# The last output bank of an encoder kernel in two column halves, and tile 2's scaling behind the last square root

## The chip, the cores and the metric

The kernel runs on one core of one Trainium2 chip. The metric is the device time of one execution in microseconds. Before the change three runs gave 1183.38, 1183.96 and 1184.81 us; their median, 1183.96, is the time before. The engines are named as in the profile: PE is TensorE's matmuls and PEld its weight loads, DVE is VectorE, ACT is ScalarE, POOL is GpSimd and SP is SyncE, which only issues DMAs here. ACT issues DMAs too.

## The reference

A two-layer pre-norm encoder on 512 tokens (an 8 by 64 grid) of width 1024, all in float32. Layer 0 mixes with two kinds of attention, layer 1 with a neighbourhood attention; each layer ends in a squared-ReLU MLP of width 4096, and the whole in an RMSNorm. Only the end matters here:

```python
def rmsnorm(x, g):
    xf = x.astype(jnp.float32)
    y = xf * lax.rsqrt(jnp.mean(xf * xf, axis=-1, keepdims=True) + EPS)
    return (y * g.astype(jnp.float32)).astype(x.dtype)

def sq_relu_mlp(h, w_up, w_down):
    u = jax.nn.relu(h @ w_up)
    return (u * u) @ w_down
...
        h = h + sq_relu_mlp(rmsnorm(h, norm_ffn[layer]), ffn_w_up[layer], ffn_w_down[layer])
    return rmsnorm(h, final_norm)
```

## The kernel before

A float32 product is made from three matmuls in a faster type: each operand is split into a high and a low part, and high times high, high times low and low times high are added up in PSUM. Most of the kernel keeps the activations transposed, features on partitions, in a tile called hT.

The end of the last MLP is different. Of its 32 blocks of 128 hidden features, the last four are not multiplied in the transposed form: they are kept back (V) and used as the stationary operand, so that the product comes out with tokens on partitions, which is how the output is stored and how the last norm sums its squares along a row. `last_mlp` does this. H holds four tiles, H[0] to H[3], each of 128 tokens by 1024 columns; G holds the final gain on all partitions; ss is a 128 x 8 tile with the sums of squares, column j for the first 512 columns of tile j and column 4 + j for the last 512.

`down(k0, c, up, tail)` makes column half c of all four tiles. It takes four PSUM banks of 128 x 512, and `use(k, j)` adds the three matmuls of hidden block k to bank j (L1627 to L1629). With c = 0, two blocks go over all four banks in turn and the last two blocks bank by bank; with c = 1 all four blocks go bank by bank, so bank 0 is finished first and bank 3 last, each after 12 matmuls of 512 columns. When a bank is finished, `add` (L1581, VectorE) adds it to H[j].

For c = 0, `first_half` then sums the squares (L1585, ScalarE, with an accumulator that a short instruction reads out), makes 1/D times the sum plus EPS in ss (L1589, VectorE) and multiplies the half by the gain (L1590, VectorE). For c = 1, `last_half` sums the squares of the second half (L1585) and finishes the tile:

- L1595, ScalarE: root, the square root of the whole mean
- L1596, VectorE: v, the mean itself
- L1597, VectorE: y, the reciprocal of the root
- L1599 to L1601, VectorE: one Newton step, a factor rf for each token
- L1603 and L1604, ScalarE: the first 512 columns times rf, then their store to DRAM (256 KB), issued from ScalarE's queue
- L1605, VectorE, and L1606, SP: the last 512 columns times rf times the gain, then their store, issued from SP's queue

Each engine takes its instructions from its own queue in a fixed order. A scheduler sets that order when the program is built, from the program's text and its dependencies; between instructions of one engine it may change the order of the text. `tc.keep_in_program_order` marks an instruction that it leaves where the text has it. Instructions of different engines wait for each other by semaphores. Around the last bank, the queue of VectorE had these in this order: L1605 of tile 1; L1596, L1597 and L1599 of tile 2; the add of tile 3 (L1581); L1600, L1601 and L1605 of tile 2; L1596 and the rest of tile 3. ScalarE's had: L1595 of tile 2; the store L1604 of tile 1; the squares of tile 3; L1603 of tile 2; L1595 of tile 3; the store of tile 2; L1603 and the store of tile 3.

Of the kernel before, what the change touches and what calls it, by code (L numbers as in the profile page):

```python
# [11 lines left out]
AF = mybir.ActivationFunctionType  # L12
ALU = mybir.AluOpType
# [3 lines left out]
S = 512  # L17
D = 1024
# [17 lines left out]
def encoder_kernel(ctx: ExitStack, tc: tile.TileContext, ins, out, dbg=None):  # L36
    nc = tc.nc
    PE, ACT, DVE, POOL, SP = nc.tensor, nc.scalar, nc.vector, nc.gpsimd, nc.sync
# [40 lines left out]
    def mmb():  # L79
        return bank("mm", 3)  # L80

    def sbk():
        return bank("s", 2)

    def stb():
        return bank("t", 2)

    def ob():
        return bank("o", 1)

    def scratch(dt=F32):
        return scp.tile([P, 512], dt, tag="sc", name=nm("sc"))

    def tiny(n, dt=F32):
        return tp.tile([P, n], dt, tag=f"ti{n}", name=nm("ti"))

    def keep(shape, dt, name):
        return big.tile(shape, dt, tag=name, name=name)
# [127 lines left out]
    def rows(w, k0, nk):  # L226
        return w[k0 * P : (k0 + nk) * P, :].rearrange("(k p) n -> p k n", p=P)
# [5 lines left out]
    def plan(*spec, make=None):  # L233
        asked.append((make or chunk, spec))
        return len(asked) - 1

    def weights(i, ahead=AHEAD):
        while len(loaded) < min(i + LOAD + 1, len(asked)):
            make, spec = asked[len(loaded)]
            loaded.append(make(*spec))  # L240
            next(loaded[-1])
        while len(ready) < min(i + ahead + 1, len(asked)):
            hi, lo, lows = next(loaded[len(ready)])
            ready.append((hi, lo))
            low_parts.append(lows)

            give_low(len(ready) - fixed[0])
        give_low(i + 1)
        return ready[i]
# [4 lines left out]
    def give_low(n):  # L254
        while given[0] < n:
            for z in low_parts[given[0]]:
                z()
            given[0] += 1
# [147 lines left out]
    def group(n):  # L406

        flip[0] ^= 1
        if flip[0]:
            return [sbk(), stb(), stb(), ob()][:n]  # L410
        return [mmb(), mmb(), mmb(), sbk()][:n]
# [232 lines left out]
    hold = {}  # L644
# [65 lines left out]
    banks = [mmb() for _ in range(3)] + [sbk(), sbk(), ob()]  # L710
# [860 lines left out]
    def last_mlp():  # L1571
        H = []
        G = []
        ss = keep([P, 8], F32, "ss")
        ov = out.rearrange("b (r c) d -> (b c) r d", r=ROWS)

        def half(j, c):
            return H[j].t[:, S * c : S * c + S]

        def add(j, c, b):  # L1580
            DVE.tensor_tensor(half(j, c), half(j, c), b, op=ALU.add)  # L1581

        def squares(j, c):
            sq = scratch()
            ACT.activation(sq, half(j, c), AF.Square, accum_out=ss[:, 4 * c + j : 4 * c + j + 1])  # L1585

        def first_half(j):
            squares(j, 0)
            DVE.tensor_scalar(ss[:, j : j + 1], ss[:, j : j + 1], 1.0 / D, EPS, op0=ALU.mult, op1=ALU.add)  # L1589
            DVE.tensor_tensor(half(j, 0), half(j, 0), G[0].t[:, 0:S], op=ALU.mult)  # L1590

        def last_half(j):
            squares(j, 1)
            v, root, a, y, rf = (tiny(1) for _ in range(5))
            ACT.activation(root, ss[:, 4 + j : 5 + j], AF.Sqrt, bias=ss[:, j : j + 1], scale=1.0 / D)  # L1595
            DVE.tensor_scalar(v, ss[:, 4 + j : 5 + j], 1.0 / D, ss[:, j : j + 1], op0=ALU.mult, op1=ALU.add)  # L1596
            DVE.reciprocal(y, root)  # L1597

            DVE.tensor_scalar(a, v, y, y, op0=ALU.mult, op1=ALU.mult)  # L1599
            DVE.tensor_scalar(a, a, -0.5, 1.5, op0=ALU.mult, op1=ALU.add)  # L1600
            DVE.tensor_tensor(rf, a, y, op=ALU.mult)  # L1601
            dst = ov[16 * j : 16 * j + 16]
            ACT.activation(half(j, 0), half(j, 0), AF.Copy, scale=rf)  # L1603
            ACT.dma_start(dst[:, :, 0:S], half(j, 0))  # L1604
            DVE.scalar_tensor_tensor(half(j, 1), half(j, 1), rf, G[0].t[:, S:], op0=ALU.mult, op1=ALU.mult)  # L1605
            SP.dma_start(dst[:, :, S:], half(j, 1))  # L1606

        def turn(i, c):

            b = stb() if flip[0] == 0 else mmb()  # L1610
            for q in range(4):
                PE.transpose(b[:, q * P : (q + 1) * P], hT[:, 4 * c + q, i * P : (i + 1) * P], ident)
            ACT.activation(half(i, c), b, AF.Copy)

        def down(k0, c, up, tail):

            nk = len(up)
            ids = [plan([(0, S, rows(ins["ffn_w_down"][1], k0 + k, 2)[:, :, S * c : S * c + S])], 2, S)
                   for k in range(0, nk, 2)]

            def run():
                banks = group(4)

                def use(k, j):
                    wh, wl = (x[:, k % 2, :] for x in weights(ids[k // 2]))
                    uh, ul = (up[k][:, z, j * P : (j + 1) * P] for z in range(2))
                    PE.matmul(banks[j], uh, wh, start=k == 0, stop=False)  # L1627
                    PE.matmul(banks[j], uh, wl, start=False, stop=False)
                    PE.matmul(banks[j], ul, wh, start=False, stop=k == nk - 1)  # L1629

                for k in range(nk - tail):
                    for j in range(4):
                        use(k, j)
                for j in range(4):
                    for k in range(nk - tail, nk):
                        use(k, j)
                    if c == 0:
                        turn(j, 1)
                    add(j, c, banks[j])
                    (first_half, last_half)[c](j)  # L1640
                    if c == 0 and j == 3:

                        ACT.activation(tiny(1), ones[:, 0:1], AF.Sqrt)

            return run

        runs, V = [], []

        def last(k0, tiles_):
            V.extend(tiles_)  # L1650
            up = [s_.pair() for s_ in V]
            runs.extend(down(k0, c, up, 2 + 2 * c) for c in range(2))

            def beside(m, i):
                if m == 2 and i == 0:
                    H.extend(Slot(F32) for _ in range(4))
                    G.append(Slot(F32))
                    SP.dma_start(G[0].t, ins["final_norm"].unsqueeze(0).to_broadcast([P, D]))
                if m > 1 and i in (16, 22):
                    turn(2 * (m - 2) + (i == 22), 0)  # L1660

            return beside

        mlp(1, last)
        for run in runs:
            run()
        for s_ in V:
            s_.free()

    last_mlp()  # L1670


# [50 lines left out]
```

## Time and profile before

| what | value |
|---|---|
| median of three runs | 1183.96 us (1183.38 to 1184.81) |
| the profiled execution's own time | 1184.41 us |
| its span, first to last instruction | 1182.3 us |
| PE matmul, busy | 1162.6 us, 98% |
| PE weight load, busy | 1018.3 us, 86% |
| VectorE, busy | 877.6 us, 74% |
| ScalarE, busy | 640.0 us, 54% |
| GpSimd, busy | 520.1 us, 44% |
| mean granted TensorE clock | 0.997 |

A profile comes from one execution. Its times count from the start of its span, in us. A timeline row gives start, duration, engine, line, operation and its tiles; a bracket at its end tells how long the engine was idle before and what released it. ACTq and SPq rows are an engine's queue issuing a DMA. The chain of waits is followed back from the last instruction of a compute engine: each row is a piece of time and what filled it, and "issue" is time in which the engine waited for nothing that the profile shows. Grouped rows give a line, its tiles and shapes, the count, then the busy time in us and the mean ns of one, then the idle time before. Rows over stretches of time give, for each stretch, its length, the busy time of each engine with its number of instructions, the granted PE clock, the busy share of the DMA engines and their GB/s. DMA rows give, per queue, packets, MB and the busy share in that stretch. The end of a matmul is modelled and matmuls overlap; the rate is read from their starts.

### The profile page before, as it was taken

What the parts mean: (1) busy time and instruction counts of PE and PEld (TensorE: products, weight loads), DVE (VectorE), ACT (ScalarE), POOL (GpSimd) and SP (SyncE); (2) the same over time, 40 slices, a digit from 0 to 9 for tenths busy, and PEclk for the clock granted to TensorE, in tenths of its full rate; (3) what the DMA queues carried; (4) which work ended last, traced back from release to release, by engine and by line L of the source; (5) the groups of instructions that cost most, each with busy time, mean ns of one, the idle gap of its engine ahead of it and who ended that gap; (6) DMA issues with size and microseconds to landing.
All of it is one profiled execution on the core that took longest, in us unless ns stands there. A gap on an engine that the chain in (4) does not pass through costs nothing.

```text
span 1182.3 us, 19765 instructions
## 1 busy us (share of the span) xinstructions
PE 1162.6 (98%) x7128; PEld 1018.3 (86%) x7128; DVE 877.6 (74%) x1506; ACT 640.0 (54%) x1081; POOL 520.1 (44%) x659
## 2 busy tenths in 40 slices
PE   9999999999999999999999999999999999999997
PEld 8667788887899899988998998988889989998895
DVE  5588998878967378786984676667995736777975
ACT  5577676764446246662543555555544524666344
POOL 3257242215662477709502232231366625774820
PEclk9999999999999999999999999999999999999998
DMA  7223314222515722225226574443352332322412
GB/s 245 73 58 92 86 54 135 72 63 81 177 56 152 253 72 82 72 91 169 63 76 174 137 180 126 115 112 109 106 162 81 116 126 62 90 72 90 143 37 71
DMA packets 110145, 128.01 MB, mean 108 GB/s; under 512 B 9075, under 2 KB 86816, under 8 KB 110048
## 3 DMA queue, kind: packets, MB, share of 16 engines
q1 hardware_dynamic: 106992, 119.30, 33.9%
q0 software_dynamic: 2304, 6.31, 2.3%
q10 hardware_dynamic: 752, 1.15, 0.3%
q8 instruction: 56, 0.92, 0.3%
q14 instruction: 41, 0.34, 0.1%
HBM read 104.32 MB, written 6.29 MB: 94 GB/s over the span
## 4 chain that ended last, share of the span: by engine, by line
PE 86%; DVE 7%; ACT 3%; issue 1%; POOL 1%; DMA 1%; SPq 0%; DVEq 0%; ACTq 0%; POOLq 0%
PE mm L503 8%; PE mm L501 8%; PE mm L502 8%; PE mm L390 3%; PE mm L389 3%; PE mm L388 3%; PE s L503 3%; PE s L501 3%; PE s L502 3%; PE t L389 3%; PE t L388 3%; PE t L390 3%; PE s L991 2%; PE s L390 2%; PE s L388 2%; PE s L389 2%
## 5 line engine op out<-in xcount | busy, mean ns | idle before, releaser
L309 DVE TENSOR_TENSOR wlo<-a,whi 128x896 fp32r<-128x896 f32 x132 | 164.5, 1251 | 83.6 <-ACT whi L308 82.8
L308 ACT ACTIVATE whi<-a 128x896 fp32r<-128x896 f32 x132 | 124.7, 949 | 152.3 <-PE o L502 45.9
L501 PE MATMUL mm<-a,whi 128*128 128x512 f32 x485 | 195.5, 405 | 0.2 <-DVE hT L925 0.2
L503 PE MATMUL mm<-a,wlo 128*128 128x512 f32 x485 | 191.9, 397 | 2.4 <-DVE wlo L202 2.4
L502 PE MATMUL mm<-a,whi 128*128 128x512 f32 x485 | 192.2, 396 | 0.1
L202 DVE TENSOR_TENSOR wlo<-raw,whi 128x1024 fp32r<-128x1024 f32 (+4 forms) x117 | 139.3, 1194 | 69.6 <-ACT whi L212 66.1
L212 ACT ACTIVATE whi<-raw 128x1024 fp32r<-128x1024 f32 (+3 forms) x120 | 116.3, 970 | 99.2 <-PE s L502 32.1
L302 POOL TENSOR_TENSOR a<-a 128x128 f32<-128x128 f32 x132 | 84.0, 636 | 171.4 <-DMA a<-in_ffn_w_up_dram 98.9
L304 POOL TENSOR_TENSOR a<-a 128x128 f32<-128x128 f32 x132 | 122.6, 928 | 10.3
L303 POOL TENSOR_TENSOR a<-a 128x256 f32<-128x256 f32 x132 | 117.5, 890 | 10.3
L503 PEld LDWEIGHTS mm<-a,wlo 128*128 128x128 f32 x485 | 91.0, 188 | 25.0 <-DVE wlo L202 2.9
L501 PEld LDWEIGHTS mm<-a,whi 128*128 128x128 f32 x485 | 91.2, 188 | 20.3 <-issue 1.4
L502 PEld LDWEIGHTS mm<-a,whi 128*128 128x128 f32 x485 | 91.4, 189 | 19.6 <-issue 1.7
L389 PE MATMUL mm<-a,whi 128*128 128x256 f32 x370 | 104.1, 281 | 0.0
L388 PE MATMUL mm<-a,whi 128*128 128x256 f32 x370 | 103.9, 281 | 0.0
L390 PE MATMUL mm<-a,wlo 128*128 128x256 f32 x370 | 103.8, 281 | 0.0
L999 POOL TENSOR_SCALAR p<-p,ti 128x512 f32<-128x512 f32 x64 | 46.1, 721 | 88.5 <-DVE ti L998 74.5
L1424 POOL TENSOR_SCALAR p<-p,ti 128x256 f32<-128x256 f32 x64 | 35.4, 564 | 105.7 <-DVE ti L1423 92.6
L388 PE MATMUL t<-a,whi 128*128 128x256 f32 x264 | 74.2, 281 | 0.0
L389 PE MATMUL t<-a,whi 128*128 128x256 f32 x264 | 74.2, 281 | 0.0
L390 PE MATMUL t<-a,wlo 128*128 128x256 f32 x264 | 73.9, 280 | 0.0
L390 PEld LDWEIGHTS mm<-a,wlo 128*128 128x128 f32 x370 | 69.7, 188 | 0.2 <-DVE wlo L309 0.2
(333 smaller groups left out, 3195.1 us busy)
## 6 DMA issues: line engine op xcount, KB each, us to landing
a<-in_ffn_w_up_dram SPq DMA_DIRECT2D x104, 256.0 KB
raw<-in_ffn_w_down_dram SPq DMA_DIRECT2D x46, 512.0 KB
raw<-in_od_w_qkv_dram SPq DMA_DIRECT2D x64, 128.0 KB
a<-in_ffn_w_down_dram SPq DMA_DIRECT2D x28, 256.0 KB
raw<-in_ffn_w_up_dram SPq DMA_DIRECT2D x12, 512.0 KB
raw<-in_ev_w_in_dram SPq DMA_DIRECT2D x12, 384.0 KB
a<-a SPq DMA_DIRECT2D x18, 256.0 KB
bias<-bx SPq DMA_DIRECT2D x16, 256.0 KB
```

Of the source, the lines that this page charges most:

```text
L202: z = lambda: (eng or DVE).tensor_tensor(to, src, f32(high), op=ALU.subtract)
L212: ACT.activation(hi[:, 0:m], raw[:, 0:m], AF.Copy)
L303: POOL.tensor_tensor(r[:, 4:6], r[:, 2:3].to_broadcast([P, 2, P]), r[:, 0:7:6], op=ALU.add)
L304: POOL.tensor_tensor(r[:, 7], r[:, 3], r[:, 5], op=ALU.subtract)
L308: ACT.activation(hi[:, 0:896], raw[:, 128:1024], AF.Copy)
L309: DVE.tensor_tensor(lo[:, 0:896], raw[:, 128:1024], f32(hi[:, 0:896]), op=ALU.subtract)
L388: PE.matmul(o, wh, x[:, 0], start=kp == 0 and n in (0, 1, 3, 5), stop=False, skip_group_check=True)
L389: PE.matmul(o, wh, x[:, 1], start=False, stop=False, skip_group_check=True)
L390: PE.matmul(o, wl, x[:, 0], start=False, stop=kp == self.np - 1, skip_group_check=True)
L501: PE.matmul(o, wh, xh, start=first, stop=False)
L502: PE.matmul(o, wh, xl, start=False, stop=False)
L503: PE.matmul(o, wl, xh, start=False, stop=last)
```

## The change

Two things are changed, both for the last bank, c = 1 and j = 3. The bank is made in two halves of 256 columns: all 12 matmuls for columns 0 to 255, then all 12 for columns 256 to 511, and after each half `last_bank` adds that half to H[3] and sums its squares. After the first half a new one-column step on VectorE adds the first sum to ss[3], so that the second sum can be written over it. And tile 2's `last_half` stops after rf: its two scalings and its two stores (`store`) are called after tile 3's `scale`, which holds the square root; the ScalarE scaling of tile 2 is marked to stay there.

```diff
-        def add(j, c, b):
-            DVE.tensor_tensor(half(j, c), half(j, c), b, op=ALU.add)
+        def add(j, c, b, o=0, n=S):
+            h = half(j, c)[:, o : o + n]
+            DVE.tensor_tensor(h, h, b[:, o : o + n], op=ALU.add)
 
-        def squares(j, c):
+        def squares(j, c, o=0, n=S):
             sq = scratch()
-            ACT.activation(sq, half(j, c), AF.Square, accum_out=ss[:, 4 * c + j : 4 * c + j + 1])
+            ACT.activation(sq[:, 0:n], half(j, c)[:, o : o + n], AF.Square,
+                           accum_out=ss[:, 4 * c + j : 4 * c + j + 1])
...
-        def last_half(j):
-            squares(j, 1)
+        def scale(j):
             v, root, a, y, rf = (tiny(1) for _ in range(5))
             ACT.activation(root, ss[:, 4 + j : 5 + j], AF.Sqrt, bias=ss[:, j : j + 1], scale=1.0 / D)
...
             DVE.tensor_tensor(rf, a, y, op=ALU.mult)
+            return rf
+
+        def store(j, rf, held=lambda z: z):
             dst = ov[16 * j : 16 * j + 16]
-            ACT.activation(half(j, 0), half(j, 0), AF.Copy, scale=rf)
+            held(ACT.activation(half(j, 0), half(j, 0), AF.Copy, scale=rf))
             ACT.dma_start(dst[:, :, 0:S], half(j, 0))
             DVE.scalar_tensor_tensor(half(j, 1), half(j, 1), rf, G[0].t[:, S:], op0=ALU.mult, op1=ALU.mult)
             SP.dma_start(dst[:, :, S:], half(j, 1))
+
+        def last_half(j):
+            squares(j, 1)
+            rf = scale(j)
+            if j == 2:
+                hold["rf"] = rf
+            else:
+                store(j, rf)
+
+        def last_bank(b, use):
+            for o in (0, 256):
+                use(o)
+                add(3, 1, b, o, 256)
+                squares(3, 1, o, 256)
+                if o == 0:
+                    DVE.tensor_scalar(ss[:, 3:4], ss[:, 7:8], 1.0 / D, ss[:, 3:4], op0=ALU.mult, op1=ALU.add)
+            rf = scale(3)
+            store(2, hold["rf"], tc.keep_in_program_order)
+            store(3, rf)
...
-                def use(k, j):
-                    wh, wl = (x[:, k % 2, :] for x in weights(ids[k // 2]))
+                def use(k, j, o=0, n=S):
+                    wh, wl = (x[:, k % 2, o : o + n] for x in weights(ids[k // 2]))
                     uh, ul = (up[k][:, z, j * P : (j + 1) * P] for z in range(2))
-                    PE.matmul(banks[j], uh, wh, start=k == 0, stop=False)
-                    PE.matmul(banks[j], uh, wl, start=False, stop=False)
-                    PE.matmul(banks[j], ul, wh, start=False, stop=k == nk - 1)
+                    b = banks[j][:, o : o + n]
+                    PE.matmul(b, uh, wh, start=k == 0, stop=False, skip_group_check=n < S)
+                    PE.matmul(b, uh, wl, start=False, stop=False, skip_group_check=n < S)
+                    PE.matmul(b, ul, wh, start=False, stop=k == nk - 1, skip_group_check=n < S)
...
                 for j in range(4):
+                    if c and j == 3:
+                        last_bank(banks[3], lambda o: [use(k, 3, o, 256) for k in range(nk - tail, nk)])
+                        break
                     for k in range(nk - tail, nk):
                         use(k, j)
```

## The prediction

> **What bounds the kernel now.** The page first: whose work stands on the chain that ended last.
>
> ```profile
> PE 86%; DVE 7%; ACT 3%; issue 1%; POOL 1%; DMA 1%; SPq 0%; DVEq 0%; ACTq 0%; POOLq 0%
> ```
>
> TensorE sets most of the span, but the change touches only what follows the last matmuls. So I read the chain of waits from there to its end, and then the timeline of the last 13 us.
>
> ```profile
> 1173.49 0.70 DVE a L1581
> ...
> 1174.21 0.72 ACT sc L1585 x2
> 1174.93 0.06 ACT a L1603
> 1174.99 0.46 issue
> 1175.45 0.29 ACT ti L1595
> ...
> 1175.76 0.17 DVE ti L1597
> ...
> 1176.65 0.75 DVE a L1605
> ```
>
> This is tile 3 (the last 128 tokens): add the bank (L1581), sum the squares (L1585), square root (L1595), four small steps, scale (L1605). Between squares and root lies 0.52 us (0.06 + 0.46) that belongs to neither: ScalarE's queue holds tile 2's scaling (L1603) there. The timeline shows it, with the last bank's matmuls and the stores:
>
> ```profile
> 1170.50 0.40 PE L1627 MATMUL s<-whi,a 128*128 128x512 f32 x1
> ...
> 1171.70 0.75 DVE L1605 SCALAR_TENSOR_TENSOR a<-a,ti,a 128x512 f32<-128x512 f32 x1
> ...
> 1172.37 0.21 DVE L1596 TENSOR_SCALAR ti<-ss 128x1 f32<-128x1 f32 x1
> ...
> 1172.69 0.28 ACT L1595 ACTIVATE ti<-ss 128x1 f32<-128x1 f32 x1
> ...
> 1173.00 0.16 DVE L1597 RECIPROCAL ti<-ti 128x1 f32<-128x1 f32 x1 [0.42 <-ACT ti L1595]
> 1173.05 0.40 PE L1629 MATMUL s<-whi,a 128*128 128x512 f32 x1
> ...
> 1174.47 0.75 DVE L1605 SCALAR_TENSOR_TENSOR a<-a,ti,a 128x512 f32<-128x512 f32 x1
> 1174.74 0.19 ACT L1585 ACTIVATION_READ_ACCUMULATOR sc<-a 128x1 f32 x1
> 1174.84 0.71 ACT L1603 ACTIVATE a<-a,ti 128x512 f32<-128x512 f32 x1
> ...
> 1175.25 0.54 SPq L1606 DMA_DIRECT2D out_dram<-a  x1
> ...
> 1175.45 0.28 ACT L1595 ACTIVATE ti<-ss 128x1 f32<-128x1 f32 x1
> 1175.57 0.55 ACTq L1604 DMA_DIRECT2D out_dram<-a  x1
> ...
> 1177.40 0.55 ACTq L1604 DMA_DIRECT2D out_dram<-a  x1
> 1177.43 0.54 SPq L1606 DMA_DIRECT2D out_dram<-a  x1
> ```
>
> PE ends the last bank at 1173.05 + 0.40 = 1173.45. The two stores of tile 3 are issued at 1177.40 (ScalarE) and 1177.43 (SP), and the span ends at 1182.30. Of the 3.95 us between, the change can reach about one: the copy's 0.52 us and half of an add and of a squares pass.
>
> **Where the last data goes.** Traffic per DMA queue in narrow windows (q1 is SP's, q10 ScalarE's), first from 1178.50 to 1179.45 (with the share of busy DMA engines in 40 slices of it, 0.024 us each), then to 1179.70, then from 1179.95 to the end:
>
> ```profile
> DMA  0000093429499887549995900499099098989299
> ...
> q10 hardware_dynamic: 84, 0.17, 82.3%
> ...
> q10 hardware_dynamic: 40, 0.06, 67.1%
> q1 hardware_dynamic: 10, 0.02, 21.4%
> ...
> q1 hardware_dynamic: 107, 0.19, 21.5%
> ```
>
> Both stores were issued within 0.03 us, yet nothing moves until the sixth slice, 1178.62; q10 then runs alone until 1179.45, and q1 starts only after that. Two 256 KB stores follow each other: the first moves data 1.2 us after its issue, the second about 0.9 us behind the first. Tile 2's pair, issued at 1175.25 and 1175.57, does likewise: from 1176.30 to 1177.25 only q1 has packets.
>
> ```profile
> q1 hardware_dynamic: 84, 0.17, 80.5%
> ```
>
> So the end hangs on the pair's earlier issue; the later one may come up to 0.9 us behind it for nothing.
>
> **The change part by part.** The order of the built program decides this more than the diff does. VectorE's queue around the last bank (names as in the kernel before):
>
> ```
> scale tile 1 (L1605)
> add tile 3, columns 0-255     (waits PE)
> v, 1/root, three steps of tile 2 (L1596 to L1601)
> scale tile 2 (L1605)
> ss[3] += ss[7]/D              (new)
> add tile 3, columns 256-511   (waits PE)
> v ... of tile 3, scale tile 3
> ```
>
> ScalarE's: square root of tile 2, store of tile 1, squares of tile 3 first half, second half, square root of tile 3, scale tile 2, store tile 2, scale tile 3, store tile 3. And PE's first matmul of the second half waits for VectorE's first half add: both halves lie in one bank.
>
> 1. *Matmuls.* Twelve 512-wide matmuls become 24 of 256. Twelve took 1173.05 - 1170.50 = 2.55 us over eleven starts, 0.232 each. For 256 columns:
>
> ```profile
> 1148.52 0.28 PE L388 MATMUL s<-a,whi 128*128 128x256 f32 x1
> ...
> 1149.11 0.28 PE L390 MATMUL s<-a,wlo 128*128 128x256 f32 x1
> ```
>
> Six such starts: 0.59 / 5 = 0.118 us, so the weight loads keep up and the work is the same. The first half ends at 1170.50 + 11 x 0.118 + 0.28 = 1172.08.
>
> 2. *First add and PE's wait.* The add stands behind tile 1's scaling (1171.70 + 0.75 = 1172.45; independent work starts 0.08 before that end, as L1596 did), so 1172.37. Price:
>
> ```profile
> L399 DVE TENSOR_TENSOR a<-a,mm 128x256 f32<-128x256 f32 x18 | 7.4, 411 | 0.0
> ```
>
> It ends at 1172.78, and PE restarts. How fast, after a pause on VectorE, and at which clock:
>
> ```profile
> 95.48 0.66 DVE L969 TENSOR_TENSOR a<-t,a 128x512 fp32r<-128x512 f32 x1
> ...
> 96.20 0.88 PEld L979 LDWEIGHTS o<-a,a 128*128 128x128 f32 x7 [1.54 <-DVE a L969]
> ...
> 95.00:96.20 1.20, 0.10 (x1) 0.00 (x0) 1.20 (x4) 1.03 (x2) 0.54 (x1) 1.00 0.57 164
> 96.20:97.30 1.10, 1.10 (x8) 1.10 (x9) 1.10 (x2) 0.00 (x0) 0.15 (x1) 1.00 0.80 274
> ```
>
> 0.06 us after the writer's end, clock 1.00 on both sides of 1.1 us of idle PE. So PE's second half runs from 1172.84 to 1172.84 + 1.30 + 0.28 = 1174.42, 0.97 us later than the bank ends now.
>
> 3. *Second add.* Tile 2's square root is untouched, so its reciprocal stays at 1173.00. Before, tile 3's add stood in the middle of tile 2's small steps; now nothing does. Tile 3's undisturbed steps took 1176.65 - 1175.76 = 0.89, so tile 2's scaling starts at 1173.89 and ends at 1174.64. The new one-column step starts at 1174.56, and the add one pair later:
>
> ```profile
> 1158.84 0.15 DVE L1589 TENSOR_SCALAR ss<-ss 128x1 f32<-128x1 f32 x1
> 1158.90 0.68 DVE L1590 TENSOR_TENSOR a<-a,a 128x512 f32<-128x512 f32 x1
> ```
>
> that is 1174.63 (bounds: 1174.42 if it were not behind the scaling, 1174.75 if it waited for the small step's end). PE's restart is covered by 0.2 us; without that cover each further 0.1 us of PE is 0.1 us of the end. The add ends at 1175.04, against 1174.18 before: the halved add comes 0.86 us later.
>
> 4. *Squares and root.* No 256-column squares exist in the trace. Nearest, ScalarE copies of the same two widths, and the 512-column squares:
>
> ```profile
> L362 ACT ACTIVATE a<-a 128x512 fp32r<-128x512 f32 x12 | 7.5, 630 | 15.4 <-DVE a L336 6.6 <-DVE a L340 5.1 <-DVE a L363 2.2
> L362 ACT ACTIVATE a<-a 128x256 fp32r<-128x256 f32 x4 | 1.6, 408 | 1.2 <-PE s L390 1.2
> L1585 ACT ACTIVATE sc<-a 128x512 f32<-128x512 f32 x8 | 5.0, 629 | 5.9 <-DVE a L1581 5.9
> ```
>
> I take 0.41 (both read SBUF at the same 512 price), with 0.36 and 0.63 as ends. Squares 1175.07 to 1175.48; the sum's read starts 0.10 before that end and takes 0.19: 1175.57. The copy is no longer in front, so the root starts at 1175.60 against 1175.45: from the add's start to the root it takes 0.97 us instead of 1.96 (0.49 for the copy, 0.28 for the add, 0.22 for the squares), and the add starts 1174.63 - 1173.49 = 1.14 us later. Sum here: +0.15. First half squares (added: 0.41 + 0.19) and the new step lie before 1174.56, under PE's second half; if uncovered they would cost 0.6.
>
> 5. *Stores.* Root ends 1175.88, tile 3's scaling on VectorE runs 1176.80 to 1177.55, SP issues at 1177.58: +0.15 on its old 1177.43, +0.18 on the pair's first issue, 1177.40. On ScalarE tile 2's scaling runs 1175.79 to 1176.51, its store occupies the queue 1176.53 to 1177.08, and behind that waits tile 3's scaling: 1177.10 to 1177.82 and its store at 1177.85 if the issue holds the queue, 0.3 earlier if not. Either is within 0.9 us of SP's, so it costs nothing. Tile 2's SP store moves from 1175.25 to 1174.67, its ScalarE store from 1175.57 to 1176.53; that one moves data from about 1177.7 to 1178.9, just ahead of SP's 1178.8.
>
> Sum: +0.18 us. Span 1182.3 becomes 1182.5, the profiled run 1184.41 becomes 1184.6. That run lies 0.45 us above the median of 1183.96 (runs 1183.38 to 1184.81), so I put the shift on the median: **1184.1 us**, which is no change: about 0.2%, 2.4 us, is what a measurement of this kernel can tell.
>
> [...]
>
> **The rivals.**
>
> *Stores run side by side* (+0.45 us, 1184.4). If each store began 1.2 us after its own issue whatever the other does, ScalarE's issue at 1177.85 instead of 1177.40 would set the end. For: queueing behind tile 2's store is certain if an issue holds ScalarE. Against: in both pairs read above the second store waits. [...]
>
> *PE's restart is late* (slower, up to +1.4 us, 1185.5). Place: the second half's twelve matmuls behind the add. It decides once they end after 1174.63, so from 0.2 us of loss on. Price at half clock: 11 x 0.236 + 0.56 = 3.16 us instead of 1.58, and 1.58 - 0.21 = 1.4. Against: clock 1.00 after the pause at 95 us. For: PE has never yet been stopped inside this product, and the 0.2 us of cover is thin.
>
> *The change does what it says* (faster, -1.0 us, 1183.0). With the second add at PE's old end: 1173.49 + 0.41, squares to 1174.34, sum to 1174.43, root at 1174.46, 0.99 us earlier. Against: VectorE's fixed order puts tile 2's scaling first, and PE waits for the first add; both would have to fall away. [...]
>
> **How the numbers follow.** Forecast 0.80; side by side 0.07; late restart 0.08; as it says 0.05. Unknown costs: squares -0.05 to +0.22, second add -0.21 to +0.12, store pair 0 to +0.27: with the +0.18, -0.1 to +0.8. A median of readings that spread by -0.58 and +0.85 adds about half of that on either side and the late restart most of its price: 1183.2 to 1185.4. All cases lie within 2.4 us, so same 0.94; slower 0.04 is a late restart met by a high reading, faster 0.02 what no row shows.
>
> **What would show it.** Right: PE idle about 0.7 us between halves; tile 2's VectorE scaling ending near 1174.6 before a 256-column add; no copy between squares and root; root starting at about 1175.6; SP's store first of the last pair, q10's data after q1's. Wrong: the second add near 1173.5, or PE's second half ending after the scaling; a gap over 0.2 us between the sum's read and the root; both queues' data starting together; any difference ahead of 1170.5, where the programs are the same.

## The result, and the profile after

| | before | after |
|---|---|---|
| median, 22 runs each on one chip | 1184.55 us (1183.26 to 1186.18) | 1186.04 us (1184.22 to 1186.95) |
| ratio, 95% interval | | 1.0014 (1.0008 to 1.0019), that is +0.9 to +2.3 us |
| profiled execution, its span | 1184.41, 1182.3 us | 1186.64, 1184.5 us |
| first matmul of the last bank | 1170.50 | 1171.87 |
| from there to the span's end | 11.80 | 12.63 |

The kernel is slower by some 0.14%, inside the 0.2% that was called no change, and above the predicted range. The last two rows part the two profiles. 1.37 us of the 2.2 arise ahead of the last bank, where the programs are the same. From here on, +x stands for x us after the first matmul of the last bank, so that kernels can be laid on each other; what the changed instructions do is the last row, +0.83. The profile gives spans to 0.1 us, so this difference, and every end read from a span below, is good to 0.05 us; from the unrounded times of the last instructions in the two traces it is +0.86.

The share of the span by engine, on the chain that ended last, is nearly what it was:

```profile
PE 86%; DVE 7%; ACT 3%; issue 2%; POOL 1%; SPq 0%; DMA 0%; ACTq 0%; DVEq 0%; POOLq 0%
```

The chain's last pieces after the change (start, length, what):

```profile
1175.26 0.75 DVE a L1610
1176.01 0.12 DVE ss L1628
1176.14 0.34 DVE a L1582
...
1176.56 0.52 ACT sc L1586 x2
1177.08 0.02 issue
1177.10 0.02 ACT ti L1597
```

The copy of tile 2 is gone from between squares and root: 0.02 us lie there, where 0.52 lay. In its place tile 2's VectorE scaling (L1610, 0.75 us) stands in front of the second add. The timeline gives both halves:

```profile
1171.87 0.28 PE L1654 MATMUL s<-whi,a 128*128 128x256 f32 x1
...
1173.17 0.27 PE L1656 MATMUL s<-whi,a 128*128 128x256 f32 x1
...
1173.74 0.41 DVE L1582 TENSOR_TENSOR a<-a,s 128x256 f32<-128x256 f32 x1
...
1174.21 0.38 PE L1654 MATMUL s<-whi,a 128*128 128x256 f32 x1 [0.76 <-DVE a L1582]
...
1174.43 0.28 PE L1655 MATMUL s<-wlo,a 128*128 128x256 f32 x1
...
1175.63 0.28 PE L1656 MATMUL s<-whi,a 128*128 128x256 f32 x1
1175.93 0.21 DVE L1628 TENSOR_SCALAR ss<-ss 128x1 f32<-128x1 f32 x1
1176.06 0.41 DVE L1582 TENSOR_TENSOR a<-a,s 128x256 f32<-128x256 f32 x1
1176.56 0.42 ACT L1586 ACTIVATE sc<-a 128x256 f32<-128x256 f32 x1 [1.26 <-DVE a L1582]
...
1177.10 0.29 ACT L1597 ACTIVATE ti<-ss 128x1 f32<-128x1 f32 x1
...
1178.04 0.55 ACTq L1609 DMA_DIRECT2D out_dram<-a  x1
...
1178.32 0.75 DVE L1610 SCALAR_TENSOR_TENSOR a<-a,ti,a 128x512 f32<-128x512 f32 x1
1178.63 0.72 ACT L1608 ACTIVATE a<-a,ti 128x512 f32<-128x512 f32 x1 [0.62 <-DVE ti L1603]
1179.38 0.55 ACTq L1609 DMA_DIRECT2D out_dram<-a  x1
```

The same timeline for SP's queue alone:

```profile
1179.09 0.54 SPq L1611 DMA_DIRECT2D out_dram<-a  x1
```

The first of the two last stores is issued at 1179.09, +7.22. Before, it was +6.90. So 0.32 of the 0.83 us are there at the issue, and 0.51 come behind it, where nothing computes but ScalarE's copy, to +7.48. The DMA traffic in 40 slices of 0.1 us, from +7.2 to +11.2, before and after:

```profile
DMA  9999940005979597998999989993100000000000
GB/s 307 328 348 410 369 144 21 0 0 164 266 143 205 102 184 184 266 348 328 369 389 328 307 328 389 410 348 123 62 0 0 0 0 0 0 0 0 0 0 0
```

```profile
DMA  0349695889884558589899899699986563311000
GB/s 0 102 143 246 123 266 102 184 266 328 328 307 164 184 164 164 123 164 246 225 307 307 246 307 287 205 369 307 348 307 246 225 246 123 123 41 41 0 0 0
```

Before, tile 2's second store ends, two slices are empty, and the last pair runs for 20 slices. After, tile 2's second store starts only at the second slice and no gap follows it: the last pair's first packets move while its last ones still do. In the 0.15 us from 1180.38 to 1180.53 of the trace after, both queues have packets, SP's of tile 3 and ScalarE's of tile 2:

```profile
q1 hardware_dynamic: 12, 0.02, 52.8%
q10 hardware_dynamic: 7, 0.00, 8.9%
```

From the packet records, the pair's first packet to its last: +8.12 to +10.12 before (2.00 us), +8.51 to +10.99 after (2.48). SP's store alone takes 2.31 us, where the first of a pair took 1.35. The 0.83 us are then: 0.32 later issue, 0.07 more from issue to first packet (1.22 and 1.29), and 0.48 longer pair, 0.87 in all; the 0.04 too much is the rounding of the spans. From the last packet to the end it is 1.68 us both times by the unrounded traces.

### The profile page after: what moved, and what is told of

The parts are those of the page before. It is cut to its first block, busy times and chain, and to the rows that moved or that the text cites. A ratio compares the mean times of both kernels' runs of the same rounds, so it can differ in the third digit from the quotient of the medians.

```text
span 1184.5 us, 19794 instructions
## 1 busy us (share of the span) xinstructions
PE 1164.0 (98%) x7140; PEld 1019.0 (86%) x7140; DVE 875.0 (74%) x1508; ACT 641.0 (54%) x1083; POOL 519.0 (44%) x659
## 4 chain that ended last, share of the span: by engine, by line
PE 86%; DVE 7%; ACT 3%; issue 2%; POOL 1%; SPq 0%; DMA 0%; ACTq 0%; DVEq 0%; POOLq 0%
PE mm L503 8%; PE mm L501 8%; PE mm L502 8%; PE mm L390 3%; PE mm L389 3%; PE mm L388 3%; PE s L503 3%; PE s L501 3%; PE s L502 3%; PE t L389 2%; PE t L388 2%; PE t L390 2%; PE s L991 2%; PE s L388 2%; PE s L389 2%; PE s L390 2%
## 5 line engine op out<-in xcount | busy, mean ns | idle before, releaser
L309 DVE TENSOR_TENSOR wlo<-a,whi 128x896 fp32r<-128x896 f32 x132 | 161.7, 1229 | 86.6 <-ACT whi L308 86.1
L302 POOL TENSOR_TENSOR a<-a 128x128 f32<-128x128 f32 x132 | 83.9, 636 | 172.9 <-DMA a<-in_ffn_w_up_dram 100.5
L304 POOL TENSOR_TENSOR a<-a 128x128 f32<-128x128 f32 x132 | 117.7, 891 | 10.3
```

The costliest lines, as they stand in the source:

```text
L304: POOL.tensor_tensor(r[:, 7], r[:, 3], r[:, 5], op=ALU.subtract)
L309: DVE.tensor_tensor(lo[:, 0:896], raw[:, 128:1024], f32(hi[:, 0:896]), op=ALU.subtract)
```

## The experiments

The theory: the last pair is long because a third store, tile 2's from ScalarE, still moves when SP's begins. The rivals: the pair's length follows from which of its stores goes first, or from something else in the halves; and, for the larger difference in the medians, that the change costs time ahead of the last bank. One table from the packet records first (times are +x; "gap" is from the last packet of tile 2's second store to the first of the last pair, negative where they overlap):

| kernel | root | pair's issues, SP / ScalarE | gap | pair: first to last packet | long | end |
|---|---|---|---|---|---|---|
| before | 4.95 | 6.93 / 6.90 | 0.21 | 8.12 to 10.12 | 2.00 | 11.80 |
| before again (e4) | 4.95 | 6.93 / 6.90 | 0.22 | 8.12 to 10.13 | 2.01 | 11.76 |
| halves only (e1) | 5.29 | 7.29 / 7.26 | 1.14 | 8.48 to 10.49 | 2.01 | 12.21 |
| move, spaced (e5) | 4.46 | 6.85 / 6.82 | 0.11 | 8.04 to 10.06 | 2.02 | 11.30 |
| move, spaced, again (e11) | 4.47 | 6.85 / 6.82 | 0.13 | 8.05 to 10.06 | 2.01 | 11.26 |
| move, spaced, SP first (e10) | 4.46 | 6.85 / 7.29 | 0.12 | 8.05 to 10.04 | 1.99 | 11.70 |
| changed, spaced (e9) | 5.23 | 7.61 / 7.58 | 0.17 | 8.81 to 10.81 | 2.00 | 12.04 |
| changed, one step, timed (e14) | 5.24 | 7.43 / 7.52 | -0.02 | 8.63 to 10.71 | 2.08 | 12.42 |
| changed, one step (e12) | 5.22 | 7.41 / 7.50 | -0.04 | 8.61 to 10.69 | 2.08 | 12.34 |
| changed, timed again (e13) | 5.23 | 7.23 / 7.51 | -0.13 | 8.53 to 11.03 | 2.50 | 12.69 |
| changed, again (e3) | 5.23 | 7.22 / 7.50 | -0.14 | 8.50 to 10.96 | 2.46 | 12.64 |
| changed (after) | 5.23 | 7.22 / 7.51 | -0.15 | 8.51 to 10.99 | 2.48 | 12.63 |
| as it says (e6) | 4.26 | 6.26 / 6.54 | -0.18 | 7.58 to 10.20 | 2.62 | 12.06 |
| move only (e2) | 4.46 | 6.46 / 6.75 | -0.21 | 7.72 to 10.44 | 2.72 | 12.26 |

A pair of 2.0 us is called regular below, one of 2.46 us or more long. The column that tests the theory is "long". The ends of e5, e11 and e9 come 0.43 us earlier for a reason apart from the data: SP's waits come in another order there (last section). A ratio below is worked out from the single runs and is not the quotient of the two medians beside it.

**Halves only (e1).** Both scalings of tile 2 stay where they were.

```diff
-            if j == 2:
-                hold["rf"] = rf
-            else:
-                store(j, rf)
+            store(j, rf)
...
-            store(2, hold["rf"], tc.keep_in_program_order)
```

> Only the first part of the change: the last bank in two halves; tile 2's scalings and stores stay where they were before. I count from the first matmul of the last bank to the end of the span: 11.80 us in the profile before, 12.63 after. Theory (the second half's add is late, because VectorE's queue has tile 2's scaling in front of it and PE waits for the first add; the extra 0.5 us behind the stores come from tile 2's late ScalarE store): second add 4.2 us after the first matmul as after, ScalarE's scaling and store of tile 2 in front of the second squares, root at about 5.2, both last stores issued at about 7.2 (before: 6.90), store pair regular again (second store's data done about 3.2 us after the pair's first issue), 12.1 us in all, so +0.3 on before. Rival (the long last transfer after the change was one execution's chance): the same 12.1 here, so this run does not tell the two apart, but it sizes the halves alone. Rival (the halves are free and the moved store makes the whole loss): 11.8.

Measured: 1185.90 us against 1185.52 before, ratio 1.0003 (0.9994 to 1.0011); the end at +12.21, 0.41 later than before. The root is 0.34 later, the pair regular:

```profile
DMA  2000000000003497959797999979995200000000
```

Halving by itself makes the end later, and its stores keep their gap. The rival that the halves are free (11.8) is out.

**Move only (e2).** The bank in one piece, as before.

```diff
-            for o in (0, 256):
-                use(o)
-                add(3, 1, b, o, 256)
-                squares(3, 1, o, 256)
-                if o == 0:
-                    DVE.tensor_scalar(ss[:, 3:4], ss[:, 7:8], 1.0 / D, ss[:, 3:4], op0=ALU.mult, op1=ALU.add)
+            use(0)
+            add(3, 1, b)
+            squares(3, 1)
```

> Only the second part: the last bank whole, 512 columns; tile 2's scalings and stores behind tile 3's square root. Theory: the root starts 0.03 us after the squares' sum is read, 4.5 us after the last bank's first matmul (before 4.95), SP's last store is issued at 6.45 (before 6.93), ScalarE's scaling of tile 3 starts only when its queue has issued tile 2's store; if three stores close to each other slow the last pair, 11.9 us in all, else 11.4. Rival (long last transfer was chance): 11.4. Rival (moving the scaling makes the loss): 12.3 or more.

Measured: 1185.94 us, ratio to before 1.0006 (0.9997 to 1.0015). The root comes 0.49 us earlier than before and the stores are issued 0.44 earlier, yet the end is 0.46 later:

```profile
DMA  9988844865989979996999756653432000000000
GB/s 307 348 307 348 307 164 164 205 123 102 225 205 266 266 225 287 246 266 205 287 266 307 205 164 246 246 205 143 164 143 82 21 0 0 0 0 0 0 0 0
```

From the sixth slice, where the pair begins, to the end no slice has over 307 GB/s, while the pair before reached 410. In the first 1.8 us of the pair the DMA engines are nearly as busy as they were in the pair before (mean digit 7.6 against 8.2) and move less (223 GB/s against 281). So the copy of tile 2 in front of the root was worth 0.49 us of the 0.52 that the profile before shows, and moving it buys a longer pair that takes back more. The theory had said 11.9 and the rival that the move makes the loss 12.3 or more; 12.26 is the rival's number, so this run alone does not speak for the overlap.

**The two kernels again (e3, e4)**, for a second profile of each.

> The changed kernel as it is, a second profile. If the long last transfer (2.3 us where others take 1.1 to 1.4) comes from the three stores, it is there again and the last bank's first matmul to the end takes 12.6 us; if it was chance, 12.15. The 1.37 us that the first profile lost ahead of the last bank, where PE's matmuls ran 0.43 us apart for 3 us behind a PE stall at 1102 us, may be there or not; if the change made it, it is there.

> The kernel before as it is, a second profile: 11.80 us from the last bank's first matmul to the end, both store pairs regular. Ahead of the last bank: if slow matmuls behind the PE stall near 1102 us are the chip's own chance, they can show here too; if the change makes them, never.

One execution each, 1186.51 and 1186.18 us. The end comes at +12.64 and +11.76, against +12.63 and +11.80: the part behind the last bank's first matmul repeats within the rounding. The start of that bank does not: 1172.24 in this profile of the kernel before, against 1170.50 in the first. The time ahead of it is taken up below.

**The move, with the pair later (e5, e11).** Two more one-column steps on VectorE, a multiplication by one, behind tile 3's factor; added to the move alone.

```diff
             rf = scale(3)
+            for _ in range(2):
+                later = tiny(1)
+                DVE.tensor_tensor(later, rf, ones[:, 0:1], op=ALU.mult)
+                rf = later
```

> The second part alone (as in the move-only kernel), with two one-column multiplications by 1.0 put between tile 3's factor and its scalings, so that the last two stores are issued about 0.4 us later. Theory (the last pair is slow because SP's store starts to move while tile 2's ScalarE store still does): the pair now starts at about 8.02 us after the last bank's first matmul, behind the end of tile 2's store at 7.93, it is regular again (1.3 and 1.1 us), and the kernel with more work ends earlier than move-only: 11.7 us instead of 12.26, even a little ahead of before (11.80). Rival (the pair is slow for another reason: SP issuing first, or two ScalarE stores in a row): still 2 us and more a store, 12.6 us.

> The same kernel as the move with the two extra steps, for a second profile and more times. Theory: the last pair regular again, its data done at 10.0 to 10.1, the span's end 11.3 to 11.8 us after the last bank's first matmul (11.76 to 11.80 in the kernel before); the time is 0 to 0.5 us less than before (ratio 0.9996 to 1.0000). Rival (the 11.30 was an accident of one profile and the pair can go either way): pair 2.5 us, end at 12.2 or later.

Work was added on the path, and the end comes a microsecond earlier than with the move alone: +11.30 and +11.26. Of this microsecond 0.38 us lie in the data, which are done at +10.06 instead of +10.44; 0.43 are the order of SP's waits, which the expected 11.7 did not have, and some 0.15 a shorter time from the last packet to SP's release, which stays unexplained. The pair is regular, here in the second of the two:

```profile
DMA  9989730057998888979998999752000000000000
```

In time: 1183.78 against 1184.38 us, and 1183.26 against 1183.95, a ratio of 0.9994 (0.9985 to 1.0003) each time. This is the best version found. That it beats the kernel before is shown by the ends (0.5 us, twice each); the times alone do not part them. Only 0.06 us of the 0.5 lie in the data, the rest in how SP waits at the end (last section).

**The change as it says (e6).** A bank of its own for the second half, so that TensorE does not wait; second add and new step ahead of tile 2's VectorE scaling.

```diff
+            held = tc.keep_in_program_order
-            for o in (0, 256):
...
+            b = sbk()
+            use(256, b)
+            held(add(3, 1, b, 256, 256))
+            held(DVE.tensor_scalar(ss[:, 3:4], ss[:, 7:8], 1.0 / D, ss[:, 3:4], op0=ALU.mult, op1=ALU.add))
+            squares(3, 1, 256, 256)
+            held(DVE.scalar_tensor_tensor(half(2, 1), half(2, 1), hold["rf"], G[0].t[:, S:], op0=ALU.mult, op1=ALU.mult))
+            SP.dma_start(ov[32:48][:, :, S:], half(2, 1))
```

> The change as the prediction's rival had it: the second half in a bank of its own (PE does not wait for the first add), and VectorE's queue with the second add and the new step in front of tile 2's scaling. Second add at 3.1 us after the last bank's first matmul (after: 4.19), root at 4.4 (before 4.95, after 5.23), SP's last store issued at 6.4 (before 6.93, after 7.22). Prediction's rival: 0.6 to 1.0 us earlier at the end than before, 11.0 to 11.2. Theory of overlapping stores: SP's last store starts at 7.6, while tile 2's ScalarE store moves until about 7.75, so the pair is slow and the end is at 11.8 to 12.1, no gain on before (11.80).

Measured, one execution: 1184.16 us. TensorE does not pause: its starts are 0.11 to 0.13 us apart through both halves. The root starts at +4.26, 0.69 earlier than before; the end is 0.26 later than before (0.21 by the unrounded traces), with a pair of 2.62 us. The prediction's rival of this name had the root 0.99 earlier; it came 0.30 short, as the second squares waited behind the new step (0.29 us idle, released by it), and the rest was lost in the stores.

**Tile 2's first scaling on GpSimd (e7)**, stored by SP, in the kernel before; then the same for tiles 0 to 2 (e8), with tile 2's VectorE scaling behind tile 3's add.

```diff
-            ACT.activation(half(j, 0), half(j, 0), AF.Copy, scale=rf)
-            ACT.dma_start(dst[:, :, 0:S], half(j, 0))
+            if j in (2,):
+                POOL.tensor_scalar(half(j, 0), half(j, 0), rf, None, op0=ALU.mult)
+                SP.dma_start(dst[:, :, 0:S], half(j, 0))
+            else:
+                ACT.activation(half(j, 0), half(j, 0), AF.Copy, scale=rf)
+                ACT.dma_start(dst[:, :, 0:S], half(j, 0))
```

> The kernel before, with the scaling of tile 2's first 512 columns on GpSimd instead of ScalarE and its store issued from SP. ScalarE's queue has neither scaling nor store of tile 2, so the root starts at 4.47 us (before 4.95) and both scalings of tile 3 start together. Theory of overlapping stores: tile 2's stores move until about 7.9 as before, the last pair would start at 7.65 and is slow, 12.0 to 12.3 us in all, though no queue is held. Rival (the loss of move-only is ScalarE's held queue or its two stores in a row): 11.3.

> As before, with the scalings of the first 512 columns of tiles 0, 1 and 2 on GpSimd and their stores on SP, and tile 2's VectorE scaling behind tile 3's add. Without tile 1's scaling in ScalarE's queue tile 2's root comes 0.5 us earlier, and so do its stores: they move until about 7.0, so the last pair at 7.65 overlaps nothing. Theory: root at 4.47, pair regular, 11.3 us, 0.5 us faster than before. Rival (GpSimd's scaling takes longer than its 0.72 us elsewhere or slows VectorE beside it): 11.8 or more.

The first tells nothing of the pair: GpSimd needed 2.13 us for the scaling that costs ScalarE 0.71, and SP's later stores queued behind it; 1186.54 us in one execution, the end at +12.69.

```profile
1175.85 2.13 POOL L1608 TENSOR_SCALAR a<-a,rf 128x512 f32<-128x512 f32 x1 [39.19 <-DVE rf L1602]
```

The second ends at +11.68, where 11.3 was expected, and takes 1185.09 us against 1184.38, ratio 0.9999 (0.9991 to 1.0008). Here tile 2 has both stores on SP's queue, so SP's packets can be told apart only by counting them; by that count, a pair that overlaps the last of them by 0.10 us took 2.04 us, its members 1.99 and 1.84. It fits neither the regular nor the long form, and stays unexplained.

**The change, with the pair later (e9, e12).** The same two steps, and then one, added to the changed kernel.

```diff
             rf = scale(3)
+            for _ in range(2):
+                later = tiny(1)
+                DVE.tensor_tensor(later, rf, ones[:, 0:1], op=ALU.mult)
+                rf = later
```

> The changed kernel with two more one-column multiplications by one behind the reciprocal's last step, so that both last stores are issued about 0.4 us later than in the changed kernel (about 7.6 us after the last bank's first matmul, instead of 7.22 and 7.51). Overlap theory (the last pair is slow because SP's last store begins to move while tile 2's ScalarE store, done at about 8.66, still moves): the pair begins behind it, at 8.7 to 9.0, takes about 2.0 us again, and the span ends 12.3 to 12.5 us after the last bank's first matmul, earlier than the 12.63 of the changed kernel although there is more work in front. Rival (the pair's length is set by something else, the delay simply adds): pair about 2.5 us, end at 12.9 to 13.0.

> The changed kernel with one extra step: both last stores issued about 0.2 us later than in the changed kernel, SP's at about 7.42, so that its data begin at about 8.7, within 0.05 us of the end of tile 2's ScalarE store (8.66). Overlap theory: hardly any overlap, a pair of 2.0 to 2.1 us, the end at 12.2 to 12.5. Rival (length set by something else): pair about 2.5 us, end at 12.8.

With two steps the pair is regular, and the data are done 0.18 us before the changed kernel's although SP's store is issued 0.39 later; the end is 0.59 earlier, the other 0.41 from the order of SP's waits, which brings it below the 12.3 to 12.5 expected. A gap is there again, in the fifteenth and sixteenth slices:

```profile
DMA  0449897879873100796969899799998997210000
```

With one step the overlap is 0.04 us and the pair 2.08 us long; SP's waits are in the changed kernel's order, the data are done 0.30 us earlier and the end is 0.29 earlier:

```profile
DMA  0469697689873168598799798988998972000000
```

The delay does not add to the end, as the rival had it; it takes away. 1184.01 us against 1183.95 before for two steps, ratio 1.0004 (0.9995 to 1.0014); 1183.94 in one execution for one step.

**SP's store first, without overlap (e10).** In every long pair SP's store had been the first as well. To the spaced move two one-column ScalarE copies are added in front of tile 3's scaling there.

```diff
+            for _ in range(2):
+                later = tiny(1)
+                ACT.activation(later, rf, AF.Copy)
+                rf = later
             ACT.activation(half(3, 0), half(3, 0), AF.Copy, scale=rf)
```

> The move with the two extra steps, and two one-column copies on ScalarE in front of tile 3's scaling there, so that SP's store of tile 3 is issued 0.3 to 0.5 us ahead of ScalarE's, but begins to move (about 8.0 us after the last bank's first matmul) only when tile 2's ScalarE store has ended (7.9). In every slow pair so far SP's store was first as well, so the two are to be told apart. Overlap theory: the pair is regular, each store 1.1 to 1.4 us, done at 10.1 to 10.4. Rival (a pair in which SP's store goes first is slow): SP's store takes 2.3 us or more, the pair 2.5 us, done at 10.5 to 10.8.

SP's store moves from +8.05, 0.12 us behind tile 2's, and takes 1.29 us; ScalarE's follows; the pair is 1.99 us long. One execution took 1184.66 us.

```profile
DMA  9898741048998787999998999941000000000000
```

So a pair with SP's store first need not be long. Over the table, the pair's length rises with it: 2.0 us with any gap, 2.08 at 0.02 to 0.04 us, 2.46 to 2.50 at 0.13 to 0.15, 2.62 and 2.72 at 0.18 and 0.21. One thing goes along with the overlap: from the issue of tile 2's ScalarE store to the pair's first issue it is 1.05 or 1.06 us in every long pair, 1.25 where the pair took 2.08 and 1.42 or more in the regular ones. Among the long pairs the length still grows with the overlap at this same distance; no run holds one fixed and moves the other over the whole range.

**The changed kernel and the one step, timed (e13, e14)**, on the same chip.

> The changed kernel once more, for a second set of times. The part behind the last bank's first matmul is 0.83 to 0.88 us longer than before in all its profiles; the first set of times showed 1.0 to 2.3 us. Theory (the excess of the first set is the slow stretch at 1103 us, which falls now into one execution and now into another, whatever the kernel): about 0.85 us over the kernel before, a ratio of 1.0003 to 1.0011, and fast ends of both sets 0.8 to 1.0 us apart. Rival (the change itself costs more ahead of the last bank): 1.3 us or more again, 1.0011 or above.

> The changed kernel with one extra step behind the last reciprocal, timed, on the same chip as the changed kernel. Theory (the pair of last stores is regular as soon as SP's begins behind tile 2's ScalarE store): 0.3 us less than the changed kernel, so about 0.55 us over the kernel before, a ratio of 1.0001 to 1.0009; its profile ends 12.3 to 12.4 us after the last bank's first matmul again, with the pair at 2.0 to 2.1 us. Rival (12.34 was an accident): 12.6 or later, pair 2.4 to 2.5.

1185.89 and 1185.07 us against 1184.81 before; ratios 1.0004 (0.9995 to 1.0013) and 1.0000 (0.9992 to 1.0009). The ends repeat, +12.69 and +12.42. The changed kernel's ratio agrees with the tail's 0.85 us (1.0007 lies in its interval, 1.0011 as well, so it leans to chance without proving it; the medians lie 1.08 us apart and the fastest runs 0.64, where 0.8 to 1.0 was expected). The profiles say more. This execution of the changed kernel started its last bank at 1170.11, 0.39 earlier than the kernel before did, and took 1184.92 us. What differs is a stretch at 1103 us, in code that both kernels share. Stretch of 1090 to 1112 us: its length, the busy times of PE, PEld, DVE, ACT and POOL with their instructions, the granted clock, DMA share, GB/s. Before, and before again:

```profile
1090.00:1112.00 22.00, 19.57 (x102) 16.29 (x101) 22.00 (x29) 7.56 (x10) 19.03 (x23) 1.00 0.43 143
```

```profile
1090.00:1112.00 22.00, 19.59 (x88) 15.88 (x87) 22.00 (x29) 6.75 (x9) 18.96 (x23) 0.92 0.43 142
```

After, and after in the timed second set:

```profile
1090.00:1112.00 22.00, 19.48 (x90) 15.81 (x89) 22.00 (x28) 6.55 (x10) 19.30 (x23) 0.92 0.43 139
```

```profile
1090.00:1112.00 22.00, 20.39 (x107) 17.01 (x106) 22.00 (x30) 7.71 (x10) 18.39 (x21) 1.00 0.45 144
```

Clock 1.00 and 0.92 occur with either kernel. In these four rows 88 and 90 matmuls fit into the 22 us at 0.92, and 102 and 107 at 1.00. In the 16 profiles the lower clock came 7 times: after, e2, e3, e4, e8, e9 and e14. It costs about 1.6 us: the second profile of the kernel before runs 0.16 us behind the first up to this stretch and 1.74 behind it from there on. What goes with it is in the last section.

## Why the prediction was wrong

Laid on the same start of the last bank (1.37 us off the times after), its steps stand so:

1. *Matmuls.* Right: starts 0.118 us apart, first half done at 1172.07, predicted 1172.08.
2. *First add and PE's wait.* Right: the add at 1172.37, PE idle for 0.76 us, restart at 1172.84, both as predicted. One thing was missed: the first matmul behind the pause took 0.38 us and held the second back to 0.22, so the half ends at 1174.54 rather than 1174.42. It lay under the cover, and cost nothing.
3. *Second add.* Right in order and cause: tile 2's scaling 1173.89 to 1174.64, the new step at 1174.56. The new step took 0.21 us, not the 0.15 of the row that it was priced by, and the add starts at 1174.69, 0.06 late.
4. *Squares and root.* 0.42 us for the squares, predicted 0.41. But they start 0.09 behind the add's end instead of 0.03, and the root comes at 1175.73, 0.13 behind the predicted 1175.60. The +0.15 was +0.28.
5. *Stores.* The issue order was right, and so was the held queue: tile 3's copy started at 1178.63, 0.04 us behind the end of tile 2's store issue. The row's bracket blames its factor, L1603, but VectorE used that factor 0.31 us earlier. The step that failed is its last: "Either is within 0.9 us of SP's, so it costs nothing", and before it "that one moves data from about 1177.7 to 1178.9, just ahead of SP's 1178.8". These two numbers already overlap by 0.1 us; measured, they overlap by 0.15. Only the later issue of ScalarE was asked for its price, not the third store in the way: the range gave the store pair 0 to +0.27. It cost 0.48 us and 0.07 more from issue to first packet, since a pair that begins under a third store takes 2.48 us instead of 2.00.

So the sum of +0.18 should have been +0.83: 0.14 from steps 3 to 5's issue times, 0.07 and 0.48 from the DMA, less 0.04 by the rounding of the spans. The measured median lies 1.90 us above the forecast (1186.04 against 1183.96 + 0.18). 0.59 of that is the kernel before, whose median over 22 runs was 1184.55 and not the 1183.96 of three; the range allowed half of the three runs' upward spread, 0.43. 0.65 is the missing part of the sum. 0.66 is left. The stretch at 1103 us adds about 1.6 us where it comes, so it would make this up if the changed kernel's 22 runs had it more often; but that is not shown. The other runs left no trace, only their mean granted clock: all six profiles at 0.996 had the stretch, of the ten at 0.997 or more one had it. 8 of the changed kernel's 22 runs are at 0.996, and 7, 5, 3 and 2 of 21 of the kernel before in the four later sets; for its runs beside the change no clock is on record. So the 0.66 stay open.

The rivals: *stores side by side* had its two stores start 1.2 us behind their own issues. They did not: ScalarE's first packet came 0.86 us behind SP's. What did happen: both stores move in the same stretch. In the 1.0 us from +9.6 to +10.6 of the trace after:

```profile
q10 hardware_dynamic: 113, 0.21, 64.7%
q1 hardware_dynamic: 35, 0.06, 15.0%
```

Before, from +9.6 on, only one queue has packets:

```profile
q1 hardware_dynamic: 81, 0.13, 35.0%
```

So in this long pair both queues have packets there, with 64.7% and 15.0% of the DMA engines' time; in the regular pair before, the two transfers follow each other but for some 0.4 us (+9.04 to +9.47). *PE's restart is late*: no, apart from the 0.12 us above; the granted clock was 1.00 from 1173.00 to 1176.00. *The change does what it says*: as argued, both of its conditions failed in the changed kernel (tile 2's scaling went first, and PE waited 0.76 us), and the experiment of that name, where neither stands in the way, ends no earlier than the kernel before.

The list of what would show it: the idle 0.7 us, the scaling before the 256-column add, no copy between squares and root, SP's store first, all as written; "any difference ahead of 1170.5" was there, 1.37 us, and comes with either kernel.

## What to carry to other kernels

When an edit makes the last transfers start earlier or closer together, price the transfers too: list which ones move at that moment, from first to last packet, and treat an overlap of even 0.15 us as unpriced. A small delay that lets the transfer in front finish can pay: 0.2 us of it (e12) brought the last data 0.30 us forward. And compare profiles from a common instruction just ahead of the change, twice each, before the difference of two spans is put down to it.

## What the runs showed of the hardware

- Two 256 KB stores take 2.0 us together, the second's first packet 0.86 to 0.93 us behind the first's (0.67 and 0.59 in the two longest pairs, e6 and e2). If a third is still moving when they start, the delay lasts beyond that overlap: 0.15 us of it cost 0.48, 0.21 us cost 0.72. Why is open; it is not overlap as such, for the two stores of a regular pair overlap too (before: ScalarE's last packet ends at +9.47, SP's first starts at +9.04). All long pairs had SP's store start into ScalarE's; the reverse was not tried.
- SP waits for the stores one semaphore after the other, and which comes first counts. Its last eight waits before, and in the spaced move again (first and last start):

```profile
L1719 SPq EVENT_SEMAPHORE  x8: 27/28/28, 1181.0 to 1181.4; - x8
```

```profile
L1750 SPq EVENT_SEMAPHORE  x8: 27/28/28, 1179.6 to 1180.3; - x8
```

  Before, the store that ends last is the first one waited for, so seven more waits of 0.06 us follow it, 0.43 us. In the spaced move it is the last one waited for, and the seven are done by then. The eight semaphores are dealt out in turn in the built program's order of its DMAs, so the order of the two last stores in it decides. That is 0.43 of the 0.5 us by which e5 and e11 end earlier than before, and 0.41 of e9's 0.59; it was read from the traces, with no run made for it. e10 bears it out: its data end when those of e5 do (+10.04 and +10.06), its last store is the first one waited for, and its end is 0.4 us later.
- A pause of TensorE can cost clock or not. Ahead of the stretch at 1103 us every profile has a wait on VectorE, in the profile after this one, followed by matmuls 0.43 us apart:

```profile
1102.39 0.50 PE L503 MATMUL mm<-a,wlo 128*128 128x512 f32 x1 [2.52 <-DVE wlo L202]
...
1103.95 0.63 PE L502 MATMUL mm<-a,whi 128*128 128x512 f32 x1
1104.38 0.63 PE L503 MATMUL mm<-a,wlo 128*128 128x512 f32 x1
```

  Pauses of 1.61 to 1.89 us (5 profiles) never cost clock, those of 2.41 to 2.68 did in 7 of 11, for 3.41 us each; the same kernel did both. The clock records in the traces show what goes with the loss. In each profile all changes of the granted clock lie on one grid of 3.41 us, and what parts the profiles is how much of the pause falls into one interval of the grid. In the seven profiles it is 2.24 to 2.52 us, and the next interval runs at 0.50 (after: 0.91 us of busy PE from 1099.89 to 1103.30, then clock 0.50 from 1103.30 to 1106.71). In the nine others a border cuts the pause and at most 1.76 us fall into one interval (before: 0.87 and 1.56). Over all recorded intervals of the 16 profiles, 1.95 us or more of idle PE were always followed by half clock, 1.76 or less never (behind the last matmul, before: 2.61 us idle, then 0.50 from 1176.11 on). In that half-rate interval the matmuls start 0.43 us apart, at clock 1.00 0.23. No pause here was a whole interval long; 2.24 us of idle PE in one were enough. The grid lies elsewhere in each execution (the first border on record is at 5.34 us before and at 4.21 after), so by these records the chance is where it falls in the pause; what sets it no run shows.
